# Two more chunks of the attention gate in the stage with seven half-size products

## The chip, the core and the metric

The kernel runs on one core of a Trainium2 chip. A core has TensorE (PE) for matrix products, VectorE (DVE), ScalarE (ACT) and GpSimd (POOL) for elementwise work, and SyncE (SP), whose queue issues most transfers. Products are written to PSUM, eight banks of 128 rows by 512 float32; the other operands lie in SBUF. The metric is the device time of one execution in microseconds. Before the change three runs gave a median of 717.32 us (716.94 to 717.59).

## The reference, cut to what matters

A decoder block on 1024 tokens and 16 meta tokens, width 1024, in float32. The normalised input h is projected at once into the pooling branch (u, its gate z), the attention (q, k, v, its gate za and forget logits f) and two gates of full width, g_pool and g_attn:

```python
h = rmsnorm(x, norm_g)
proj = jnp.einsum('bld,dn->bln', h, w_in)
u_pool, z_pool, q, k, v, z_attn, f_logit, g_pool, g_attn = jnp.split(proj, _split_points(), axis=-1)
y_pool = causal_multiscale_pool(u_pool, pool_w, pool_scale) * jax.nn.silu(z_pool)
y_attn = forgetting_attention(q, k, v, log_f).reshape(B, L, ATTN_WIDTH) * jax.nn.silu(z_attn)
merged = (jax.nn.sigmoid(g_pool) * jnp.einsum('blc,cd->bld', y_pool, w_up_pool)
          + jax.nn.sigmoid(g_attn) * jnp.einsum('blc,cd->bld', y_attn, w_up_attn))
return x + jnp.einsum('bld,de->ble', merged, w_out)
```

The gate projection g_attn has 1024 columns, eight chunks of 128. The case is where each of these chunks is computed.

## The kernel before, in words

Float32 operands are split into a high and a low part, and each product is made of three: high by high, high by low, low by high. A chunk of 128 columns over the 1024 tokens takes two halves of 512 tokens, each of 8 x 3 matmuls (`g_proj`, `g_mm3`, L221). Its weights come in one 512 KB load, are split by two instructions of ACT (L208) and four of POOL (L212), and `f_raw` evicts the result by ACT (L405) and stores it to DRAM (`spill`).

**Attention.** There are 16 units: four pairs of heads, two heads each, two halves of 512 queries. Units alternate between narrow ones (first half, five blocks of 128 keys) and wide ones (second half, nine). Per block, `qk` (L738, L739) makes the scores, ACT moves them out of PSUM (L743), VectorE keeps a running maximum (L752); `maxes` brings the maximum to all rows; `soft` subtracts it (L779), takes exp (L780), splits the result into high (L784, ACT) and low (L785, VectorE), and `av` (L803) multiplies both by V. `merged` interleaves the score steps of the next unit with the softmax steps of this one.

**Fill.** TensorE would wait in all of this, so a planner (`Fill`) puts other products between: the q, k and v projections of the next pair (which must be ready at the pair's boundary, `until`), and freely the four chunks of u, the eight of g_pool and chunks 0 to 3 of g_attn (`raws`). After every step it pulls matmuls worth `PACE * dve - pe`, with its own estimates of VectorE's and TensorE's time of the step; inside `maxes` and between the last steps it pulls fixed amounts (`LM1`, `LM2`, `LATENCY`). What is left when the last unit ends is drained. The order of TensorE is that of the program; the other engines are ordered by the scheduler in this part.

**The stage with seven products.** za, z and chunks 4 to 7 of g_attn are computed after it as one 1024 by 1024 by 1024 product cut into 2 x 2 blocks, by a scheme that takes seven products of half size in place of eight. Its weight matrix stands side by side from z and gate columns: in the left half za and gate chunks 4 and 5, in the right half z and gate chunks 6 and 7 (`GB`). Sums of its blocks are made ahead by DRAM copies and accumulating transfers (`GS`, 768 columns: 512 and 256), sums of h by `HS`. The list `order` names the chunks: product n of 0 to 6, chunk i of 0 to 5, with i below 4 for za and z and 4 and 5 for the gate. One entry (n, i) is 12 matmuls of 512 columns (L1079, `g_prod`). Step x of the loop splits the weights of entry x + 4 (`w_split`: ACT L1034, then POOL L1041 or, every third time, VectorE L1038), issues the product of entry x + 2, evicts entry x - 1 (`evict`, L1084, L1090), and does the extra work that `before` and `extra` name for the entry: softmax sums, pooling chains, the splits of h (L1050, L1055), the loads of the reciprocal sums (`rc_in`) and the division (`attn_norm`). All engines keep the program's order in this stage. Weights come in pairs of chunks, 512 KB each (`pairs`, L1022): two buffers hold them, from entry (2, 0) on two more. A buffer is free for the next load when both of its chunks are split. Gate results are kept in `XE` between products, staged in `st` and stored to DRAM; `g_flush` puts the stores on SP's queue at every third step. The last four entries follow the loop, in turn with the pooling's products (`pool_mm`).

After it come the two up-projections (`up`), which read the gates back from DRAM, and the output projection (L1405) in seven half-size products of its own.

Of the kernel before, what the change touches and what calls it, by code (L numbers as in the profile page):

```python
# [33 lines left out]
PACE = 1.32  # L34
LATENCY = 1800.0
LAT2 = 1600.0
LM1, LM2 = 1400.0, 3200.0
# [16 lines left out]
def tile_hybrid_block(ctx, tc, x, meta, norm_g, w_in, b_forget, pool_w, pool_scale,  # L54
# [93 lines left out]
    GS = {n: dr.tile([512, 768], F32, name=f"gs{n}") for n in (1, 2, 3, 4, 5)}  # L148
    GB = {f"{r + 1}{c + 1}": (w_in[0][512 * r:512 * r + 512, z:z + 512], w_in[0][512 * r:512 * r + 512, g:g + 256])
          for r in range(2) for c, (z, g) in enumerate(((COL_ZA, COL_GA + 512), (COL_Z, COL_GA + 768)))}  # L150
# [498 lines left out]
    for j in range(4, 8):  # L649
        spill["ga", j] = dr.tile([128, SEQ], F32, name=f"sp_ga{j}")  # L650
# [46 lines left out]
    def gsrc(n, q):  # L697
        if n in (2, 3, 5, 6):
            return GSRC[n][:, {"a": 0, "b": 256, "g": 512}[q]:][:, :256]
        return GSRC[n][1] if q == "g" else GSRC[n][0][:, 256 * (q == "b"):][:, :256]  # L700
# [134 lines left out]
    raws = [(n, j) for n, c in (("gp", 8), ("ga", 4)) for j in range(c)]  # L835
# [181 lines left out]
    def pairs_in():  # L1017
        while pairs and room:
            e = pairs.pop(0)
            homes[e] = tag = room.pop(0)  # L1020
            raw_w[e] = (wp if tag == "raw" else hq).tile([128, 4, 256], F32, name="graw", tag=tag)
            nc.sync.dma_start(raw_w[e], rows_of(gsrc(*e)))  # L1022
# [6 lines left out]
    def w_split(e):  # L1029
        n, i = e  # L1030
        raw = raw_w[n, "aabbgg"[i]][:, :, 128 * (i % 2):][:, :, :128]
        op = bp.tile([128, 2, 4, 128], F32R, name="gw", tag="y", bufs=6)
        op_w[e] = op
        ins = nc.scalar.activation(op[:, 0], raw, AF.Copy)  # L1034
        if not splits[0]:
            after(ins, evacs[-1])
        if splits[0] % 3 == 2:
            nc.vector.tensor_tensor(op[:, 1], raw, r32(op[:, 0]), op=ALU.subtract)  # L1038
        else:
            for k in (0, 2):  # L1040
                nc.gpsimd.tensor_tensor(op[:, 1, k:k + 2], raw[:, k:k + 2], r32(op[:, 0, k:k + 2]), op=ALU.subtract)  # L1041
        splits[0] += 1
# [22 lines left out]
    order = [(n, i) for n in range(7) for i in {5: (3, 2, 1, 0, 4, 5), 6: (4, 5, 3, 2, 1, 0)}.get(n, range(6))]  # L1065
# [47 lines left out]
    def evict(e):  # L1113
        n, i = e
        ps = onto[e]
        if i < 4:
            if n == 0:
                keep(za[i][:, T0_], ps)
            elif n == 1:
                plus_(za[i][:, T0_], ps)  # L1120
            elif n == 2:
                keep(zp[i][:, T0_], ps)
            elif n == 3:
                keep(zp[i][:, T1_], ps)
            elif n == 4:
                plus_(zp[i][:, T0_], ps)
                pool_tt(zp[i][:, T0_], zp[i][:, T0_], zp[i][:, T1_], ALU.add)
                defer(3, lambda: silu(zp[i][:, T0_], zp[i][:, T0_], -1.0))
            elif n == 5:
                plus_(zp[i][:, T1_], ps)  # L1130
                defer(1, lambda: silu(zp[i][:, T1_], zp[i][:, T1_], -1.0))
            else:
                silu(za[i][:, T1_], ps)
            return
        x, r = [t[:, i - 4] for t in XE]
        if n == 0:
            keep(x, ps)
        elif n in (1, 6):
            st = stage()
            plus_(st, ps, x)  # L1140
            g_store(i, T0_ if n == 1 else T1_, st)
        elif n == 2:
            plus_(x, ps)
        elif n == 3:
            keep(r, ps)
        elif n == 4:
            st = stage()
            plus_(st, ps, x)
            plus_(st, r)
            g_store(i + 2, T0_, st)  # L1150
        else:
            plus_(x, ps)
            pool_tt(r, r, x, ALU.add)
            g_store(i + 2, T1_, r)
# [4 lines left out]
    U = {}  # L1159
# [5 lines left out]
    pairs = [(0, "g")] + [(n, q) for n in range(1, 7) for q in {5: "bag", 6: "gba"}.get(n, "abg")]  # L1165
# [11 lines left out]
    def split_next(e):  # L1177
        w_split(e)
        q = e[0], "aabbgg"[e[1]]
        halves[q] = halves.get(q, 0) + 1  # L1180
        if halves[q] == 2:
# [18 lines left out]
    def steps_of(g):  # L1200
# [5 lines left out]
        (1, 3): [open_hq, lambda: h_split(2), lambda: pad_hq()],  # L1206
# [6 lines left out]
        (0, 4): [lambda: acc_sum(3)],  # L1213
# [12 lines left out]
        (3, 3): [lambda: pool_split(3), lambda: rc_in(0), lambda: rc_in(1)],  # L1226
# [4 lines left out]
        (4, 2): [lambda: rc_in(2)],  # L1231
        (4, 3): [lambda: attn_norm(0)],
        (4, 4): [lambda: attn_norm(1)],
        (4, 5): [lambda: pool_split(1), lambda: rc_in(3)],
        (5, 3): [lambda: h_split(6)],
        (5, 2): [lambda: attn_norm(2)],
        (5, 0): [lambda: silu(za[0][:, T0_], za[0][:, T0_])],
        (5, 4): [lambda: attn_norm(3), lambda: silu(za[1][:, T0_], za[1][:, T0_]),
                 lambda: silu(za[2][:, T0_], za[2][:, T0_])],
        (5, 5): [lambda: pool_split(0)],  # L1240
# [5 lines left out]
    for x, e in enumerate(order[:38]):  # L1246
# [3 lines left out]
        if 4 <= x + AH < 42:  # L1250
            split_next(order[x + AH])
        if x + 2 < 38:
# [3 lines left out]
        run_due(x)  # L1256
        if x:
            evict(order[x - 1])
        if x % 3 == 2:
            g_flush()  # L1260
# [264 lines left out]
```

## Time and profile before

| | |
|---|---|
| median of three runs | 717.32 us |
| profiled execution, its own time | 716.32 us |
| its span, first to last instruction | 714.6 us |
| TensorE busy | 705.5 us, 99% |
| VectorE, ACT, POOL busy | 73%, 59%, 48% |
| granted TensorE clock, mean | 0.997 |
| last attention product to the first product of the stage | 413.15 to 424.38 us |
| first product of the stage to the first pooling product | 424.38 to 528.04 us |

A group's row gives line, engine and operation, output from inputs, shape and count, then busy time, mean duration in ns, and the idle time of the engine before it with what ended it. A matmul's busy time runs to its modelled end and overlaps the next, so that the rate of matmuls is read from their starts. A row of the timeline begins with start and duration in us.

### The profile page before, as it was taken

The numbers are of one execution on the slowest core, as the hardware profiler recorded it, in microseconds if no ns is written. First come the engines' busy times: TensorE is split into PE (matmuls) and PEld (weight loads), VectorE is DVE, ScalarE is ACT, GpSimd is POOL, SyncE is SP. The second block draws the span as 40 slices with busy tenths as digits, with TensorE's granted clock in tenths as the row PEclk, the third lists the DMA queues.
The fourth block names the chain that finished last, engine by engine and source line by source line (L and its number), as shares of the span: only waits on it lengthen the run. The fifth ranks groups of instructions, "written<-read, shape, count | busy, mean of one in ns | idle before, by whom it ended". The sixth has DMA issues, their size and how long they took to land.

```text
span 714.6 us, 10896 instructions
## 1 busy us (share of the span) xinstructions
PE 705.5 (99%) x3613; PEld 609.5 (85%) x3613; DVE 520.2 (73%) x916; ACT 420.4 (59%) x928; POOL 345.8 (48%) x465
## 2 busy tenths in 40 slices
PE   8999999999999999999999999999999999999996
PEld 6997999998899888898888888888888888888885
DVE  5784488576788867797677847986957554988775
ACT  7663577676767778777676623446556332535445
POOL 5413447476285837656297743355972011007152
PEclk9999999999999999999999999999999999999998
DMA  9459977956534485455656459689917466761006
GB/s 307 128 198 373 323 270 178 217 123 155 113 106 100 133 220 119 133 133 111 170 169 201 108 191 350 181 221 288 269 45 262 130 231 220 262 236 60 0 1 235
DMA packets 95354, 129.89 MB, mean 182 GB/s; under 512 B 11457, under 2 KB 62657, under 8 KB 93266
## 3 DMA queue, kind: packets, MB, share of 16 engines
q1 hardware_dynamic: 91776, 110.32, 48.2%
q0 software_dynamic: 2224, 16.25, 12.2%
q10 hardware_dynamic: 1298, 2.63, 1.0%
q8 instruction: 28, 0.46, 0.3%
q14 instruction: 28, 0.23, 0.1%
HBM read 102.25 MB, written 58.39 MB: 225 GB/s over the span
## 4 chain that ended last, share of the span: by engine, by line
PE 92%; DVE 4%; ACT 2%; issue 1%; POOL 0%; POOLq 0%; ACTq 0%; DVEq 0%
PE pj L221 52%; PE pj L1079 12%; PE pj L1405 8%; PE po L803 5%; PE pt L1079 4%; PE pt L1405 2%; PE ps L739 2%; PE ps L738 2%; PE pj L599 1%; DVE pl L785 1%; PE pj L739 1%; PE pt L283 1%; PE pj L738 1%; ACT qa L319 1%; DVE ql L323 1%
## 5 line engine op out<-in xcount | busy, mean ns | idle before, releaser
L221 PE MATMUL pj<-hh,whi 128*128 128x512 f32 (+3 forms) x576 | 127.1, 347 | 0.6 <-DVE ql L323 0.3
L221 PE MATMUL pj<-hh,wlo 128*128 128x512 f32 (+3 forms) x576 | 127.2, 346 | 0.0
L221 PE MATMUL pj<-hl,whi 128*128 128x512 f32 (+3 forms) x576 | 126.8, 345 | 0.0
L212 POOL TENSOR_TENSOR wlo<-raw,whi 128x256 fp32r<-128x256 f32 x100 | 76.1, 791 | 65.4 <-ACT whi L208 34.5
L221 PEld LDWEIGHTS pj<-hh,whi 128*128 128x128 f32 x576 | 97.2, 188 | 11.3 <-ACT hh L285 0.5
L221 PEld LDWEIGHTS pj<-hh,wlo 128*128 128x128 f32 x576 | 96.8, 188 | 10.0
L221 PEld LDWEIGHTS pj<-hl,whi 128*128 128x128 f32 x576 | 96.5, 188 | 9.7
L793 POOL TENSOR_TENSOR acc<-acc,S 128x256 f32<-128x256 f32 (+2 forms) x128 | 90.6, 727 | 8.3 <-ACT S L780 4.4
L785 DVE TENSOR_TENSOR pl<-S,ph 128x512 fp32r<-128x512 f32 (+4 forms) x112 | 80.0, 736 | 15.6 <-ACT ph L784 15.3
L1041 POOL TENSOR_TENSOR gw<-graw,gw 128x256 fp32r<-128x256 f32 x52 | 49.1, 968 | 50.1 <-ACT gw L1034 41.9
L1079 PE MATMUL pj<-gh,gw 128*128 128x512 f32 x276 | 64.3, 389 | 0.0
L1079 PEld LDWEIGHTS pj<-gh,gw 128*128 128x128 f32 x276 | 51.8, 188 | 10.8
L752 DVE TENSOR_TENSOR pt<-pt,S 128x400 f32<-128x400 f32 (+2 forms) x96 | 46.6, 485 | 19.7 <-ACT S L743 17.6
L780 ACT ACTIVATE S<-S 128x512 f32<-128x512 f32 (+4 forms) x112 | 50.2, 481 | 12.7 <-DVE S L779 12.5
L784 ACT ACTIVATE ph<-S 128x512 fp32r<-128x512 f32 (+4 forms) x112 | 52.5, 482 | 3.2 <-PE po L803 2.2
L779 DVE TENSOR_TENSOR S<-S,pt 128x512 f32<-128x512 f32 (+4 forms) x112 | 50.0, 499 | 0.6
L1034 ACT ACTIVATE gw<-graw 128x512 fp32r<-128x512 f32 x38 | 23.3, 624 | 33.6 <-DMA graw<-gs 20.2
L1297 DVE TENSOR_TENSOR rl<-pj,rl 128x512 f32<-128x512 f32 x32 | 22.0, 689 | 27.7 <-PE pj L221 27.4
L793 POOL TENSOR_TENSOR acc<-S 128x256 f32<-128x256 f32 (+1 forms) x32 | 29.5, 948 | 23.6 <-ACT S L780 20.5
L743 ACT ACTIVATE S<-ps,negc 128x16 f32<-128x16 f32 (+4 forms) x65 | 33.0, 513 | 11.5 <-PE ps L739 10.9
L803 PE MATMUL po<-ph,V 128*128 128x512 f32 (+4 forms) x112 | 36.4, 325 | 0.0
L1405 PE MATMUL pj<-opw 128*128 128x512 f32 (+1 forms) x168 | 36.2, 374 | 0.0
(250 smaller groups left out, 1395.9 us busy)
## 6 DMA issues: line engine op xcount, KB each, us to landing
raw<-in_w_in_dram SPq DMA_DIRECT2D x27, 512.0 KB, 6.2
gs<-in_w_in_dram SPq DMA_DIRECT2D x15, 512.0 KB, 8.3
gs<-gs POOLq DMA_DIRECT2D x4, 1536.0 KB, 13.0
graw<-gs SPq DMA_DIRECT2D x12, 512.0 KB, 8.3
td<-in_w_out_dram SPq DMA_DIRECT2D x10, 512.0 KB, 9.9
graw<-in_w_in_dram SPq DMA_DIRECT2D x9, 512.0 KB, 5.7
xt<-in_x_dram SPq DMA_DIRECT2D x8, 512.0 KB, 6.4
accd<-acc SPq DMA_DIRECT2D x16, 256.0 KB, 2.5
```

What stands on the lines that cost most here:

```text
L212: ins = nc.gpsimd.tensor_tensor(lo[:, k:k + 2], raw[:, k:k + 2], r32(hi[:, k:k + 2]), op=ALU.subtract)
L221: nc.tensor.matmul(ps, a, b, start=(i == 0), stop=(i == len(seq) - 1))
L752: nc.vector.tensor_tensor(m[:kb, c0:], m[:kb, c0:], s[:kb, c0:], op=ALU.max)
L779: nc.vector.tensor_tensor(s[:kb, c0:], s[:kb, c0:], self.pm[:kb, c0:], op=ALU.subtract)
L780: exps.append(nc.scalar.activation(s[:kb, c0:], s[:kb, c0:], AF.Exp))
L784: nc.scalar.activation(ph[:kb, c0:], s[:kb, c0:], AF.Copy)
L785: dves.append(nc.vector.tensor_tensor(pl[:kb, c0:], s[:kb, c0:], r32(ph[:kb, c0:]), op=ALU.subtract))
L793: accs.append(nc.gpsimd.tensor_tensor(acc[:kb, c:c1], (S0 if b == 1 else acc)[:kb, c:c1], s[:kb, c:c1], op=ALU.add))
L803: nc.tensor.matmul(self.po[:, c0:], v, self.P[b][i][:kb, c0:], start=(b == 0 and i == 0), stop=(b == self.nb - 1 and i == 1))
L1041: nc.gpsimd.tensor_tensor(op[:, 1, k:k + 2], raw[:, k:k + 2], r32(op[:, 0, k:k + 2]), op=ALU.subtract)
L1079: nc.tensor.matmul(ps, stat(n, i, p, k), op_h[n][q][k // 2][:, k % 2], start=fresh and m == 0, stop=m == 11, skip_group_check=True)
L1405: nc.tensor.matmul(ps, pick(A_, k, p)[:, i * 128:(i + 1) * 128], pick(B_, k, q)[:, c0:c1], start=start and n == 0, stop=n == 11, skip_grou ...
```

## The change

Gate chunks 2 and 3 leave the fill and join the stage: `GB` and `GS` grow from 768 to 896 columns, with gate chunks 2 to 4 in the left half and 5 to 7 in the right. Each of the seven products gets a seventh entry i = 6, loaded by itself in a 256 KB piece `"e"` that takes a buffer alone. Its partial results live in one more tile of the pool `g` (`X6`), which also serves as its stage. The planner's `PACE` goes from 1.32 to 1.2 and `LM2` from 3200 to 2600. Stores are flushed at each step, ahead of the eviction. Some extra work is named for other entries: the loads of the reciprocal sums come later, as does the last division, and the last pooling split goes behind the loop. The gate's signs in `up` follow the new halves.

```diff
-PACE = 1.32
+PACE = 1.2
-LM1, LM2 = 1400.0, 3200.0
+LM1, LM2 = 1400.0, 2600.0
...
-    GS = {n: dr.tile([512, 768], F32, name=f"gs{n}") for n in (1, 2, 3, 4, 5)}
-    GB = {f"{r + 1}{c + 1}": (w_in[0][512 * r:512 * r + 512, z:z + 512], w_in[0][512 * r:512 * r + 512, g:g + 256])
-          for r in range(2) for c, (z, g) in enumerate(((COL_ZA, COL_GA + 512), (COL_Z, COL_GA + 768)))}
+    GS = {n: dr.tile([512, 896], F32, name=f"gs{n}") for n in (1, 2, 3, 4, 5)}
+    GB = {f"{r + 1}{c + 1}": (w_in[0][512 * r:512 * r + 512, z:z + 512], w_in[0][512 * r:512 * r + 512, g:g + 384])
+          for r in range(2) for c, (z, g) in enumerate(((COL_ZA, COL_GA + 256), (COL_Z, COL_GA + 640)))}
...
     def gsrc(n, q):
+        c0, w = {"a": (0, 256), "b": (256, 256), "g": (512, 256), "e": (768, 128)}[q]
         if n in (2, 3, 5, 6):
-            return GSRC[n][:, {"a": 0, "b": 256, "g": 512}[q]:][:, :256]
-        return GSRC[n][1] if q == "g" else GSRC[n][0][:, 256 * (q == "b"):][:, :256]
+            return GSRC[n][:, c0:c0 + w]
+        return GSRC[n][1][:, c0 - 512:c0 - 512 + w] if q in "ge" else GSRC[n][0][:, c0:c0 + w]
...
-    raws = [(n, j) for n, c in (("gp", 8), ("ga", 4)) for j in range(c)]
+    raws = [(n, j) for n, c in (("gp", 8), ("ga", 2)) for j in range(c)]
...
-    order = [(n, i) for n in range(7) for i in {5: (3, 2, 1, 0, 4, 5), 6: (4, 5, 3, 2, 1, 0)}.get(n, range(6))]
+    order = [(n, i) for n in range(7) for i in {5: (3, 2, 1, 0, 4, 5, 6), 6: (4, 5, 6, 3, 2, 1, 0)}.get(n, range(7))]
...
-        x, r = [t[:, i - 4] for t in XE]
+        x, r = [t[:, i - 4] for t in XE] if i < 6 else [X6[0][:, T0_], X6[0][:, T1_]]
         if n == 0:
             keep(x, ps)
         elif n in (1, 6):
-            st = stage()
+            st = stage() if i < 6 else (r if n == 1 else x)
             plus_(st, ps, x)
-            g_store(i, T0_ if n == 1 else T1_, st)
+            g_store(i - 2, T0_ if n == 1 else T1_, st)
...
-    pairs = [(0, "g")] + [(n, q) for n in range(1, 7) for q in {5: "bag", 6: "gba"}.get(n, "abg")]
+    pairs = [(n, q) for n in range(7) for q in {0: "ge", 5: "bage", 6: "geba"}.get(n, "abge")]
...
-        (1, 3): [open_hq, lambda: h_split(2), lambda: pad_hq()],
+        (1, 4): [open_hq, lambda: h_split(2), lambda: pad_hq()],
...
-        (0, 4): [lambda: acc_sum(3)],
+        (0, 4): [lambda: X6.append(gp.tile([128, SEQ], F32, name="gxe", tag="g")), lambda: acc_sum(3)],
...
-        (3, 3): [lambda: pool_split(3), lambda: rc_in(0), lambda: rc_in(1)],
+        (3, 3): [lambda: pool_split(3)],
+        (3, 6): [lambda: rc_in(0), lambda: rc_in(1)],
...
-        (4, 2): [lambda: rc_in(2)],
-        (4, 5): [lambda: pool_split(1), lambda: rc_in(3)],
+        (4, 5): [lambda: pool_split(1)],
+        (4, 6): [lambda: rc_in(2)],
-        (5, 2): [lambda: attn_norm(2)],
+        (5, 2): [lambda: attn_norm(2), lambda: rc_in(3)],
-        (5, 4): [lambda: attn_norm(3), lambda: silu(za[1][:, T0_], za[1][:, T0_]),
+        (5, 4): [lambda: silu(za[1][:, T0_], za[1][:, T0_]),
-        (5, 5): [lambda: pool_split(0)],
+        (5, 6): [lambda: attn_norm(3)],
...
         run_due(x)
+        g_flush()
         if x:
             evict(order[x - 1])
-        if x % 3 == 2:
-            g_flush()
...
-        evict((6, i + 1) if n else (6, 5))
+        evict((6, i + 1) if n else (6, 6))
+        if n == 0:
+            pool_split(0)
```

More of the change, by code (lines that the diff above doesn't have):

```diff
@@ L647, in tile_hybrid_block @@
         spill["y", p] = dr.tile([128, SEQ if p == 3 else 2 * SEQ], F32, name=f"sp_y{p}")
-    for j in range(4, 8):
+    for j in range(2, 8):
         spill["ga", j] = dr.tile([128, SEQ], F32, name=f"sp_ga{j}")
@@ L1020, in pairs_in @@
             homes[e] = tag = room.pop(0)
-            raw_w[e] = (wp if tag == "raw" else hq).tile([128, 4, 256], F32, name="graw", tag=tag)
+            raw_w[e] = (wp if tag == "raw" else hq).tile([128, 4, 128 if e[1] == "e" else 256], F32, name="graw", tag=tag)
             nc.sync.dma_start(raw_w[e], rows_of(gsrc(*e)))
@@ L1030, in w_split @@
         n, i = e
-        raw = raw_w[n, "aabbgg"[i]][:, :, 128 * (i % 2):][:, :, :128]
+        raw = raw_w[n, "aabbgge"[i]][:, :, 128 * (i % 2):][:, :, :128]
         op = bp.tile([128, 2, 4, 128], F32R, name="gw", tag="y", bufs=6)
@@ L1149, in evict @@
             plus_(st, r)
-            g_store(i + 2, T0_, st)
+            g_store(i + 1, T0_, st)
         else:
@@ L1153, in evict @@
             pool_tt(r, r, x, ALU.add)
-            g_store(i + 2, T1_, r)
+            g_store(i + 1, T1_, r)
     for i in range(4):
@@ L1158, in tile_hybrid_block @@
     XE = [bp.tile([128, 2, 512], F32, name=n, tag="xe", bufs=2) for n in ("gx", "ge")]
-    U = {}
+    U, X6 = {}, []
     def u_in(g):
@@ L1178, in split_next @@
         w_split(e)
-        q = e[0], "aabbgg"[e[1]]
+        q = e[0], "aabbgge"[e[1]]
         halves[q] = halves.get(q, 0) + 1
-        if halves[q] == 2:
+        if halves[q] == (1 if q[1] == "e" else 2):
             room.append(homes[q])
@@ L1245, in tile_hybrid_block @@
         split_next(e)
-    for x, e in enumerate(order[:38]):
+    for x, e in enumerate(order[:45]):
         if x == 0:
@@ L1249, in tile_hybrid_block @@
             g_prod(order[1])
-        if 4 <= x + AH < 42:
+        if 4 <= x + AH < 49:
             split_next(order[x + AH])
-        if x + 2 < 38:
+        if x + 2 < 45:
             g_prod(order[x + 2])
@@ L1286, in up @@
         wh, wl = ws[:2]
-        ins = nc.scalar.activation(sg_, sg_, AF.Sigmoid, scale=-1.0 if a and j > 5 else 1.0)
+        ins = nc.scalar.activation(sg_, sg_, AF.Sigmoid, scale=-1.0 if a and j > 4 else 1.0)
         after(ins, evacs[-1])
```

## The prediction

> **What bounds the kernel now.** I read the page's totals first, then the busy times by stage, then TensorE's own order of time, then what the side engines wait for.
>
> ```profile
> span 714.6 us, 10896 instructions
> PE 705.5 (99%) x3613; PEld 609.5 (85%) x3613; DVE 520.2 (73%) x916; ACT 420.4 (59%) x928; POOL 345.8 (48%) x465
> L221 PE MATMUL pj<-hh,whi 128*128 128x512 f32 (+3 forms) x576 | 127.1, 347 | 0.6 <-DVE ql L323 0.3
> L1079 PE MATMUL pj<-gh,gw 128*128 128x512 f32 x276 | 64.3, 389 | 0.0
> ```
>
> TensorE is busy 99% of the span, and its two largest groups waited 0.6 us together. By stage (columns: busy PE, weight loads, DVE, ACT, POOL, clock, DMA share, GB/s), the attention, the fill left behind it, the gate stage, one wide and one narrow attention unit:
>
> ```profile
> 60.00:413.00 353.00, 352.80 (x1896) 315.11 (x1894) 263.67 (x569) 246.64 (x614) 210.35 (x290) 1.00 0.64 169
> 413.00:424.40 11.40, 11.40 (x54) 9.45 (x53) 6.60 (x6) 1.79 (x3) 3.37 (x3) 1.00 0.59 186
> 424.40:528.00 103.60, 103.60 (x457) 85.61 (x456) 80.99 (x79) 51.95 (x82) 59.88 (x62) 1.00 0.79 238
> 191.50:207.50 16.00, 16.00 (x77) 13.51 (x76) 15.12 (x26) 14.49 (x33) 13.56 (x17) 1.00 0.41 105
> 168.90:185.00 16.10, 16.10 (x79) 13.43 (x77) 9.13 (x20) 11.48 (x25) 6.41 (x11) 1.00 0.67 171
> ```
>
> No stage leaves TensorE idle. VectorE is 75% busy over the attention, but 15.12 of 16.00 us in the softmax of a wide unit (nine key blocks) and 9.13 of 16.10 in a narrow one (five). So the bound is TensorE's stream everywhere, and the nearest other limit is VectorE in the wide units.
>
> **The price of a matmul.** A busy matmul overlaps its neighbours, so I price by the distance of starts:
>
> ```profile
> 413.15 0.48 PE L221 MATMUL pj<-hh,wlo 128*128 128x512 f32 x1
> 413.46 2.01 PE L221 MATMUL pj<-hh,whi 128*128 128x512 f32 x8
> 422.57 1.98 PE L221 MATMUL pj<-hh,wlo 128*128 128x512 f32 x8
> 424.38 1.07 PE L1079 MATMUL pj<-hh,gw 128*128 128x512 f32 x4
> 528.04 0.39 PE L221 MATMUL pj<-plh,pwh 128*128 128x512 f32 x1
> ```
>
> From 413.46 to 424.38 run 48 matmuls, the last chunk of the gate (two halves of 24): 10.92 us, 227.5 ns each. It stands behind the last attention product, as pure drain. From 424.38 to 528.04 run the 38 half-size products of the loop, 456 matmuls: 103.66 us, 227.3 ns each, 2.73 us a product. The Trainium skill (TensorE: Matmul & The Clock Gate, section Back-to-back issue gap) gives N/2.4 + 2.5 ns, 216 ns at 512 columns, for a lone stream, and about 131 ns for sustained pairs of weight load and matmul; by the second the net below would be 12 × 0.131 = 1.6 us, but the 227 ns of this trace lie by the first, and the measurement decides.
>
> **The change, part by part.** *Removed from the fill:* chunks 2 and 3, 2 × 48 = 96 matmuls, 2 × 10.92 = 21.84 us; with them two 512 KB weight loads, four splits on ACT, eight on POOL, four evictions and their stores, all beside TensorE's work. *Added to the gate stage:* a seventh product in each of the seven, 7 × 12 = 84 matmuls, 84 × 0.2273 = 19.09 us. **Net on TensorE: −2.75 us.** Beside it the gate stage gains seven splits, nine passes over evicted tiles and seven 256 KB loads (as many stores as the fill had):
>
> ```profile
> L1038 DVE TENSOR_TENSOR gw<-graw,gw 128x512 fp32r<-128x512 f32 x12 | 10.5, 877 | 5.4 <-ACT gw L1034 5.4
> L1041 POOL TENSOR_TENSOR gw<-graw,gw 128x256 fp32r<-128x256 f32 x52 | 49.1, 968 | 50.1 <-ACT gw L1034 41.9
> L1090 DVE TENSOR_TENSOR zp<-pj,zp 128x512 f32<-128x512 f32 x6 | 3.8, 679 | 1.9 <-PE pj L1079 1.9
> L1034 ACT ACTIVATE gw<-graw 128x512 fp32r<-128x512 f32 x38 | 23.3, 624 | 33.6 <-DMA graw<-gs 20.2
> L976 DVE TENSOR_TENSOR pll<-u,plh 128x1024 fp32r<-128x1024 f32 x4 | 6.5, 1615 | 1.2 <-ACT plh L975 1.2
> ```
>
> VectorE: three more splits (every third is its own) and six adds, 3 × 0.877 + 6 × 0.679 = 6.7 us. POOL: four splits of two and one add of two, 10 × 0.968 = 9.7 us. ACT: seven splits and two evictions, about 9 × 0.624 = 5.6 us. The stage grows by 19.1 us, so each lies beside TensorE: 0. If that cover failed, the longest, POOL's, would cost up to 9.7 us.
>
> *The moved steps.* The division row of head pair 2 is loaded two products ahead of its use instead of five:
>
> ```profile
> rc<-recs SPq DMA_DIRECT2D x8, 256.0 KB, 6.1
> ```
>
> Two products are 5.5 us, so VectorE may wait about 0.6 us, with evictions queued behind whose banks TensorE wants again several products later: 0, at worst 0.6. The last pooling split goes into the tail, ACT and VectorE (1.6 us), three turns of 18 matmuls (4.1 us each) ahead of its use: 0, at worst 1.6. Flushing stores at each step puts SP's weight loads behind more waits for evictions; I take that up with the loads below. The bigger copies and sums through DRAM (896 columns for 768) have the attention as cover.
>
> **What pays for it: the pace.** Two of the planner's constants fall, so that less fill is spread over all units. I followed its sums in the code (fill pulled = pace × VectorE estimate − own matmuls). For before they leave 49 matmuls to the drain, as the rows above show (1 + 48). For after they leave 26. A narrow unit then carries about 11.8 us of planned fill for 13.2, a wide one 13.8 for 15.4; one wide unit at a head-pair boundary carries 24.6 for 15.5, since the next pair's values must be ready. So TensorE arrives at each wide unit's second products earlier: 0.6 us from the shorter wait after the maxima, and 0.12 (1.32 − 1.2) of the 7.3 us that the planner estimates for the blocks passed by the sixth, 0.9 us; together 1.5 us there, and 1.8 at the unit's end. Whether it then waits is read from the lead of VectorE there. The low part of the sixth block (400 columns) and the matmul that reads it, in three wide units:
>
> ```profile
> 287.04 0.62 DVE L785 TENSOR_TENSOR pl<-S,ph 128x400 fp32r<-128x400 f32 x1
> 287.80 0.37 PE L803 MATMUL po<-pl,V 128*128 128x400 f32 x1
> 204.63 1.06 DVE L785 TENSOR_TENSOR pl<-S,ph 128x400 fp32r<-128x400 f32 x1
> 206.68 0.34 PE L803 MATMUL po<-pl,V 128*128 128x400 f32 x1
> 366.89 0.93 DVE L785 TENSOR_TENSOR pl<-S,ph 128x400 fp32r<-128x400 f32 x1
> 370.99 0.34 PE L803 MATMUL po<-pl,V 128*128 128x400 f32 x1
> 284.61 1.39 DVE L323 SCALAR_TENSOR_TENSOR ql<-pj,qa 64x512 fp32r<-64x512 f32 x2 [1.50 <-ACT qa L319]
> ```
>
> The leads are 0.14, 0.99 and 3.17 us. Less 1.5, they become stalls of 1.4 and 0.5 us and a lead of 1.7: 1.9 us if these two alone fall short and their fill stays as it is. It doesn't: the tightest comes from VectorE standing 1.50 us behind a query chunk of the fill, and the planner now puts that chunk wholly into the narrow unit before. Bounds: 0 (no stall, all leads rearranged) and 4 us (both stalls, and 0.3 us in each of the six other wide units). I take 1.0, nearer the low end, as the largest stall loses its cause. A narrow unit leaves VectorE 7 us, which covers its loss.
>
> **Sum.** The profiled execution took 716.32 us, 1.7 beyond its span and 1.0 under the median of 717.32. 716.32 − 2.75 + 1.0 = 714.57; with the 1.0 to the median, **715.5 us**.
>
> **The rivals.** *A, the sum as it stands:* stalls under 1.3 us, about 715.5. For it: every lead but two that I show is longer than what is taken.
>
> *B, the stalls eat the gain:* 1.3 to 4.2 us of them, mid 2.7, time 717.3. For it: the two short leads as they are (1.9 us). Against it: the moved query chunk.
>
> *C, slower: VectorE becomes the bound in the wide units.* It has 0.88 us free in 16.00 there, and 1.5 are taken. Should the fill's new places leave four of the wide units without a lead, each stalls 1.5 us: 6.0, time 717.32 − 2.75 + 6.0 = 720.6. It decides from 4.2 us of stalls in all. Its durations can grow too:
>
> ```profile
> L785 DVE TENSOR_TENSOR pl<-S,ph 128x512 fp32r<-128x512 f32 x48 | 44.1, 937 | 13.5 <-ACT ph L784 13.4
> L1276 DVE TENSOR_TENSOR wlu<-rawu,whu 128x512 fp32r<-128x512 f32 x15 | 10.2, 683 | 0.0
> ```
>
> The same subtraction takes 937 ns beside a busy POOL and 683 beside an idle one. The Trainium skill (SBUF — State Buffer, section Who interferes with whom) says that a VectorE operation with two SBUF inputs and a GpSimd one that reads SBUF exclude each other; the two rows agree, and by it a denser attention makes VectorE's operations longer. Against C: narrow units reset the lead.
>
> *D, the gate stage's loads come late.* The single chunk takes a whole one of two buffers, so until two more open there are four loads per 19.1 us instead of three per 16.4:
>
> ```profile
> ACT gw L1034 <- DMA graw<-gs: 20.2, 6, 5.8
> 473.01 0.63 ACT L1034 ACTIVATE gw<-graw 128x512 fp32r<-128x512 f32 x1 [5.80 <-DMA graw<-gs]
> 479.08 3.11 PE L1079 MATMUL pj<-gh,gw 128*128 128x512 f32 x13
> SPq L1000 <- DMA sums<-ge: 9.2, 1, 9.2
> ```
>
> ACT already waited 5.80 us for one load, and its split ended 5.4 us before its product (479.08). Each round of four loads loses up to 2.7 us of that, twice before the buffers open, and the read of the softmax sums then holds SP's queue for 9.2 us, the later loads behind it: 0 stall if the lead was 5.4 or more, some 4 us if all stood in a row, 718.6 with A's 1.0. I take 0.
>
> **Chances.** A 0.47, B 0.26, C 0.16, D 0.11, of which half ends within 0.2% (1.43 us, about what a measurement of this kernel tells from no change) and half above. So faster (under 715.9) 0.47, within 0.31, slower (over 718.8) 0.22. The likeliest is A. The range runs from 713.9, A without a stall and half a microsecond of scatter, to 720.3, just short of C's price.
>
> **What would show it.** Right: fill matmuls 96 fewer, gate matmuls 84 more at 2.73 us a product, drain of 26. The stalls would stand as idle time before the second attention products, released by VectorE or ACT, in wide units. D would stand as idle time before gate products released by a split. Wrong: idle TensorE over 4 us in either stage, or the distance of starts moving off 227 ns.

## The result and the profile after

The changed kernel takes 723.81 us (median of 4 runs, 722.95 to 724.13) against 717.13 (716.38 to 717.59) for the kernel before beside it: ratio 1.0092, 95% interval 1.0075 to 1.011. It is slower; I had forecast 715.5 us with 713.9 to 720.3, and the time lies above the range. Lines behind the function `gsrc` are one higher than before (L803 is now L804, L1079 is L1080).

The totals of the changed kernel's page:

```profile
span 721.2 us, 10911 instructions
PE 706.5 (98%) x3601; PEld 606.5 (84%) x3601; DVE 521.7 (72%) x925; ACT 419.2 (58%) x929; POOL 346.5 (48%) x467
```

Twelve matmuls fewer, as planned, and a span 6.6 us longer. The busy times of the changed kernel by stage (columns as in the prediction: attention, rest of the fill, gate loop to the first pooling product):

```profile
60.00:407.00 347.00, 341.44 (x1830) 302.18 (x1828) 261.15 (x570) 241.40 (x609) 203.58 (x283) 1.00 0.66 174
407.00:411.46 4.46, 4.46 (x21) 3.67 (x20) 4.36 (x5) 0.00 (x0) 0.00 (x0) 1.00 0.95 295
411.46:534.18 122.72, 122.72 (x542) 101.42 (x541) 85.74 (x88) 56.70 (x90) 71.46 (x74) 1.00 0.75 229
```

In the attention TensorE now stands idle for 347.00 − 341.44 = 5.56 us, where it was 0.2; over 4 us was the sign that the prediction had named against itself. The gate loop has no idle time at all. Its two ends on TensorE, in order of time:

```profile
411.46 1.07 PE L1080 MATMUL pj<-hh,gw 128*128 128x512 f32 x4
...
534.16 0.40 PE L221 MATMUL pj<-plh,pwh 128*128 128x512 f32 x1
```

With the same two rows of before (424.38 and 528.04) the 6.6 us divide cleanly. *The gate loop* takes 122.70 us for 103.66: +19.04. *Behind it* lie 721.2 − 534.16 = 187.04 us, 186.56 before: +0.5. *Ahead of it* its first product starts 12.92 us earlier; the 96 matmuls that left the fill are worth 21.84, so 8.92 us were lost there. −12.92 + 19.04 + 0.5 = +6.6. Below, "lost before the stage" is this quantity: the start of the stage's first product, less 424.38 us, plus 21.84 where two chunks have left the fill. (The part ahead of the attention is in it too: the first score product starts at 82.69 us before and between 82.23 and 83.72 in the other profiled executions, so that two of them can differ by 1.5 us before the attention begins.)

TensorE's waits in the attention of the changed kernel (engine, output and line, what it waited for: us in all, times, longest):

```profile
PE pj L739 <- ACT S L744: 1.6, 1, 1.6
PE po L804 <- ACT ph L785: 1.0, 1, 1.0
PE ps L739 <- DVE ka L342: 1.0, 1, 1.0
PE pj L221 <- DVE ka L342: 0.7, 1, 0.7
PE pj L739 <- DVE S L748: 0.5, 1, 0.5
PE ps L739 <- ACT S L744: 0.5, 1, 0.5
```

The view shows idle time only. By the distances of starts, in which a wait isn't shortened by the modelled end of the matmul before it, 14 stalls of 0.14 to 1.79 us make 7.9 us of the 8.92; the kernel before has one, of 0.37. I sort them by what TensorE waited for: *score products* (L739) for a bank whose evictions (L744, L748) are late, 7 stalls, 3.8 us, of which two, 1.3 us near 95 and 101 us, turn out below to be the work of the transfers; *key chunks of the fill* (the next matmuls wait for VectorE's L342), 2 stalls, 2.0 us; *the first products of wide units* (L804, high part from ACT L785), 2 stalls, 1.3 us; *the second products* (low part from VectorE L786), 2 stalls, 0.5 us; and one of 0.25 behind V's split (L367). The prediction had priced the fourth kind, the second products, alone.

Four places of the changed kernel in order of time. First the fourth kind, the one of the prediction, in the wide unit whose lead was 0.99 us (204.63 in the prediction's rows):

```profile
196.55 0.56 DVE L786 TENSOR_TENSOR pl<-S,ph 128x400 fp32r<-128x400 f32 x1
...
197.16 0.45 PE L804 MATMUL po<-pl,V 128*128 128x400 f32 x1
```

The matmul starts 0.05 us after its operand, so the lead lost 0.94 us, and TensorE had stalled 0.39 us here and 0.14 two products earlier: 1.47 us together, the 1.5 that the prediction took for such a unit.

Second, a key chunk:

```profile
226.10 1.16 PE L221 MATMUL pj<-hh,wlo 128*128 128x272 f32 x8
227.94 1.11 PE L221 MATMUL pj<-hh,whi 128*128 128x384 f32 x5 [0.68 <-DVE ka L342]
230.02 0.47 PE L739 MATMUL ps<-qa,ka 128*128 128x512 f32 x1 [0.96 <-DVE ka L342]
...
226.67 1.12 DVE L342 TENSOR_TENSOR ka<-pj,ka 64x384 fp32r<-64x384 f32 x2
227.83 1.52 DVE L780 TENSOR_TENSOR S<-S,pt 128x512 f32<-128x512 f32 x3
229.38 0.96 DVE L342 TENSOR_TENSOR ka<-pj,ka 64x256 fp32r<-64x256 f32 x3
```

The chunk's own evictions stand in VectorE's queue between softmax passes of a new unit (L780), and the next piece and the next score product want their banks. From 224 to 232 us VectorE is busy 7.02 of 8.00 us, ACT 7.28 and POOL 7.50:

```profile
224.00:232.00 8.00, 6.35 (x41) 5.74 (x40) 7.02 (x16) 7.28 (x18) 7.50 (x10) 1.00 0.72 211
```

Over the whole unit (220.1 to 244.5 us) VectorE is busy 19.36 of 24.40 us, ACT 17.31 and POOL 16.00; over these 8 us all three are nearly full.

Third, the wide unit whose lead was the shortest, 0.14 us (287.04 there):

```profile
274.70 2.41 ACT L319 ACTIVATE qa<-pj 64x512 fp32r<-64x512 f32 x4
277.01 0.62 ACT L785 ACTIVATE ph<-S 128x512 fp32r<-128x512 f32 x1
...
279.86 0.50 PE L804 MATMUL po<-ph,V 128*128 128x512 f32 x1 [0.98 <-ACT ph L785]
```

The query chunk that stood ahead of VectorE in the middle of this unit (284.61 in the prediction's rows) is in another place, as the prediction said, but that place is ACT's queue at the start of the same unit: 2.41 us ahead of the first high part. In the kernel before, that place held another query chunk, which followed the first two high parts instead of preceding them:

```profile
273.09 0.63 ACT L784 ACTIVATE ph<-S 128x512 fp32r<-128x512 f32 x1
...
274.67 0.61 ACT L784 ACTIVATE ph<-S 128x512 fp32r<-128x512 f32 x1
275.19 2.39 ACT L319 ACTIVATE qa<-pj 64x512 fp32r<-64x512 f32 x4
```

TensorE now stalls 1.29 us in two pieces, 0.14 and 1.15.

Fourth, the largest, in a narrow unit:

```profile
370.10 3.06 POOL L212 TENSOR_TENSOR wlo<-raw,whi 128x256 fp32r<-128x256 f32 x4
373.11 1.40 POOL L794 TENSOR_TENSOR acc<-S 128x256 f32<-128x256 f32 x2
374.59 2.59 POOL L794 TENSOR_TENSOR acc<-acc,S 128x256 f32<-128x256 f32 x4
...
371.80 4.30 DVE L786 TENSOR_TENSOR pl<-S,ph 128x512 fp32r<-128x512 f32 x2
376.27 0.22 ACT L781 ACTIVATE S<-S 128x16 f32<-128x16 f32 x1 [3.23 <-DVE S L780]
378.20 0.50 PE L739 MATMUL pj<-qa,ka 128*128 128x512 f32 x1 [1.62 <-ACT S L744]
```

Two of VectorE's subtractions take 4.30 us; by the single records the first of them takes 3.27, and no other of this line in either kernel takes over 1.3. It stands beside a train of POOL operations without a gap. ACT waits 3.23 us for VectorE's next pass, its own eviction (L744) comes late, and TensorE stalls 1.79 us. The Trainium skill (SBUF — State Buffer, section Who interferes with whom) says that a VectorE operation with two SBUF inputs contends with a GpSimd one that reads SBUF, for a pair of ports that is locked exclusively. The trace agrees as far as the subtraction is long beside POOL's train: it lasted while five POOL operations began (372.20 to 374.59 us). How long such a wait can last that section doesn't say, and no run here separates the ports from another cause.

### The profile page after: what moved, and what is told of

It is laid out like the page before. It is cut to its first block, busy times and chain, and to the rows that moved or that the text cites. A ratio compares the mean times of both kernels' runs of the same rounds, so it can differ in the third digit from the quotient of the medians.

```text
span 721.2 us, 10911 instructions
## 1 busy us (share of the span) xinstructions
PE 706.5 (98%) x3601; PEld 606.5 (84%) x3601; DVE 521.7 (72%) x925; ACT 419.2 (58%) x929; POOL 346.5 (48%) x467
## 4 chain that ended last, share of the span: by engine, by line
PE 84%; DVE 7%; ACT 3%; DMA 2%; issue 2%; POOL 1%; POOLq 0%; SPq 0%; ACTq 0%
PE pj L221 43%; PE pj L1080 14%; PE pj L1408 8%; PE pt L1080 5%; PE po L804 5%; PE pt L1408 2%; DMA raw<-in_w_in_dram 2%; PE ps L740 1%; PE ps L739 1%; DVE S L780 1%; PE pj L599 1%; DVE pl L786 1%; PE pt L283 1%; PE pj L739 1%; ACT qa L319 1%
## 5 line engine op out<-in xcount | busy, mean ns | idle before, releaser
L221 PE MATMUL pj<-hh,whi 128*128 128x512 f32 (+3 forms) x544 | 121.1, 346 | 1.0 <-DVE ka L342 0.7
L221 PE MATMUL pj<-hl,whi 128*128 128x512 f32 (+3 forms) x544 | 119.4, 343 | 0.0
L221 PE MATMUL pj<-hh,wlo 128*128 128x512 f32 (+3 forms) x544 | 117.5, 342 | 0.0
L212 POOL TENSOR_TENSOR wlo<-raw,whi 128x256 fp32r<-128x256 f32 x92 | 68.9, 805 | 74.7 <-ACT whi L208 58.5
L221 PEld LDWEIGHTS pj<-hh,whi 128*128 128x128 f32 x544 | 90.7, 188 | 10.6 <-PE pj L221 0.9
L221 PEld LDWEIGHTS pj<-hh,wlo 128*128 128x128 f32 x544 | 90.7, 188 | 8.4
L786 DVE TENSOR_TENSOR pl<-S,ph 128x512 fp32r<-128x512 f32 (+4 forms) x112 | 77.2, 709 | 11.5 <-ACT ph L785 11.2
L1042 POOL TENSOR_TENSOR gw<-graw,gw 128x256 fp32r<-128x256 f32 x60 | 56.0, 959 | 48.8 <-ACT gw L1035 45.8
L1080 PE MATMUL pj<-gh,gw 128*128 128x512 f32 x312 | 72.8, 389 | 0.0
L1080 PEld LDWEIGHTS pj<-gh,gw 128*128 128x128 f32 x312 | 58.6, 188 | 12.2
L785 ACT ACTIVATE ph<-S 128x512 fp32r<-128x512 f32 (+4 forms) x112 | 52.2, 484 | 2.4 <-PE po L804 1.4
L780 DVE TENSOR_TENSOR S<-S,pt 128x512 f32<-128x512 f32 (+4 forms) x112 | 50.1, 498 | 0.7
L1298 DVE TENSOR_TENSOR rl<-pj,rl 128x512 f32<-128x512 f32 x32 | 22.0, 688 | 27.6 <-PE pj L221 27.3
L744 ACT ACTIVATE S<-ps,negc 128x512 f32<-128x512 f32 (+4 forms) x67 | 33.8, 512 | 8.0 <-PE ps L740 7.7
L804 PE MATMUL po<-ph,V 128*128 128x512 f32 (+4 forms) x112 | 36.8, 329 | 1.0 <-ACT ph L785 1.0
## 6 DMA issues: line engine op xcount, KB each, us to landing
gs<-gs POOLq DMA_DIRECT2D x4, 1792.0 KB, 13.8
td<-in_w_out_dram SPq DMA_DIRECT2D x10, 512.0 KB, 10.8
```

The source lines that it names most:

```text
L212: ins = nc.gpsimd.tensor_tensor(lo[:, k:k + 2], raw[:, k:k + 2], r32(hi[:, k:k + 2]), op=ALU.subtract)
L221: nc.tensor.matmul(ps, a, b, start=(i == 0), stop=(i == len(seq) - 1))
L780: nc.vector.tensor_tensor(s[:kb, c0:], s[:kb, c0:], self.pm[:kb, c0:], op=ALU.subtract)
L785: nc.scalar.activation(ph[:kb, c0:], s[:kb, c0:], AF.Copy)
L786: dves.append(nc.vector.tensor_tensor(pl[:kb, c0:], s[:kb, c0:], r32(ph[:kb, c0:]), op=ALU.subtract))
L804: nc.tensor.matmul(self.po[:, c0:], v, self.P[b][i][:kb, c0:], start=(b == 0 and i == 0), stop=(b == self.nb - 1 and i == 1))
```

## The experiments

All ratios are against the kernel before, run beside them. The third column is defined above; the stage is from its first product to the first pooling product; the fill is what the planner's sums give a narrow and a wide unit.

| kernel | ratio, 95% interval | lost before the stage | stage | fill, us |
|---|---|---|---|---|
| before | 1 | 0 | 103.66 | 13.2, 15.4 |
| after | 1.0092 (1.0075 to 1.011) | 8.9 | 122.70 | 11.8, 13.8 |
| before, both constants | 1.0104 (1.0086 to 1.0122) | 8.7 | 103.66 | 11.8, 13.8 |
| before, PACE 1.2 alone | 1.0092 (1.0063 to 1.0121) | 4.7 | 103.66 | 12.3, 14.4 |
| before, LM2 2600 alone | 1.0048 (1.0029 to 1.0067) | 2.6 | 105.90 | 12.6, 14.7 |
| before, wider copies | 1.0063 (1.0038 to 1.0088) | 4.0 | 105.89 | 13.2, 15.4 |
| before, five early copies | 1.000 (0.9987 to 1.0013) | 0.6 | 103.66 | 13.2, 15.4 |
| after, chunks also in the fill | 1.0298 (1.0278 to 1.0318) | 3.7 | 122.70 | 13.2, 15.4 |
| after, old constants | 1.0077 (1.0054 to 1.0101) | 6.9 | 124.55 | 13.2, 15.4 |
| after, five early copies | 1.0072 (1.0045 to 1.0098) | 7.4 | 122.70 | 11.8, 13.8 |
| after, 1.35 and 2400 | 1.0006 (0.9997 to 1.0016) | 3.8 | 122.69 | 12.6, 14.8 |
| after, values in parts, 1.32 and 2800 | 1.006 (1.0038 to 1.0081) | 7.7 | 122.73 | 12.7, 15.1 |
| the same, five early copies | 1.0032 (1.002 to 1.0044) | 5.8 | 122.73 | 12.7, 15.1 |
| after, 1.35 and 2400, five early copies | 0.9983 (0.9968 to 0.9998) | 3.0 | 122.69 | 12.6, 14.8 |
| after, 1.35 and 2400, three early copies | 0.9976 (0.9961 to 0.9991) | 2.1 | 122.69 | 12.6, 14.8 |
| after, 1.28 and 2800, five early copies | 0.9983 (0.9968 to 0.9998) | 3.8 | 122.71 | 12.5, 14.7 |
| after, 1.38 and 2200, five early copies | **0.9971 (0.9956 to 0.9985)** | 1.6 | 122.79 | 12.5, 14.9 |

Two theories stood against each other. *P*: the stalls come from the lower pace and the new places of the fill. *T*: they come from the transfers, the copies through DRAM of 896 columns for 768.

**The constants alone, on the kernel before.**

```diff
-PACE = 1.32
+PACE = 1.2
-LM1, LM2 = 1400.0, 3200.0
+LM1, LM2 = 1400.0, 2600.0
```

> The kernel before with only the planner's two constants changed (PACE 1.2, LM2 2600); four gate chunks stay in the fill, the stage and the copies stay as they were. By the planner's sums 122 matmuls (27.7 us) are then left to the drain. Theory P (the lower pace makes the stalls: TensorE comes to the softmax's results before they are ready): the attention stalls as in the changed kernel, about 8 us more than before, so 725 us (722 to 727), the stalls as idle time ahead of score and second attention products. Theory T (the wider copies and sums through DRAM, or the stage, make them): neither is changed here, so 717 us.

Measured 725.45 us. P holds: with no chunk moved and no copy widened, 8.7 us are lost, and most stalls stand where the changed kernel has them; those near 95 and 101 us are missing. In their stead the clock fell here after the two waits at the key chunk, 0.64 and 0.96 us of idle time (windows of this kernel; the column behind POOL's is the granted clock):

```profile
226.00:228.00 2.00, 1.11 (x5) 0.82 (x5) 1.94 (x5) 1.93 (x7) 2.00 (x4) 1.00 1.50 493
228.00:232.00 4.00, 3.61 (x12) 3.45 (x13) 1.49 (x7) 2.79 (x8) 3.92 (x7) 0.62 0.29 70
```

The mean clock of these 4 us was 0.62; by windows of 1 us it stood at 0.50 from 229 to 232, and at 0.98 and 0.81 in the windows next to them. Nine matmuls from the score product behind the wait (228.39 to 231.25) took 2.86 us; the same nine in the changed kernel (230.02 to 231.84) took 1.82 at full clock. By the time the clock was back, the same stretch had taken 4.24 us here (to 232.63) and 2.70 there (to 232.72): 1.5 of the 8.7 us are the half clock's, and 7.2 are left for the waits.

**Each constant by itself.** The first alone, and the second alone, on the kernel before.

> Edit: the kernel before with the first constant alone as in the kernel after (1.2 for 1.32; 3200 stays), no other change; 113 matmuls are left to the drain instead of 49, which costs TensorE nothing by itself. If the lower pace between the blocks makes most of the 8 us that both constants cost on this kernel: 722 to 724 (ratio 1.007 to 1.009). By the prediction's split (0.9 us of lead in a wide unit of 1.5 is the pace's): 4.8 us of the 8, ratio 1.0065.

> Edit: the kernel before with the second constant alone as in the kernel after (2600 for 3200; 1.32 stays); 58 matmuls left to the drain. By the prediction's split (0.6 us of lead in a wide unit of 1.5): 3.2 us of the 8, ratio 1.0045. If the losses come only where both leads are used up together: under 1.002.

Measured 722.96 and 720.52 us, ratios 1.0092 and 1.0048. Before the stage they lose 4.7 and 2.6 us, near the 4.8 and 3.2 of the prediction's split; the total of the first is above it, with a wide interval. The second loses another 2.2 us in the gate stage of its profiled execution, on which see below, so that the fit of its total (1.0048 for 1.0045) is in part luck. Together the two lose 7.3 us, close to the 7.2 of waits that both constants cost at once. With the table's last column this is one series: less fill in a pair of units (28.6, 27.3, 26.7, 25.6 us), more lost (0, 2.6, 4.7, 8.7). Both have a stall near 102 us (0.95 and 0.49 us) without wider copies, so a stall at that place isn't by itself a sign of the copies.

**The old constants on the kernel after.**

```diff
-PACE = 1.2
+PACE = 1.32
-LM1, LM2 = 1400.0, 2600.0
+LM1, LM2 = 1400.0, 3200.0
```

> The changed kernel with the old constants (PACE 1.32, LM2 3200). Theory P: up to the fourteenth unit no more stalls than before; then the fill has run dry (9.9 us of planned fill missing in the last wide unit) and TensorE waits there for VectorE, about 7 us, all of it after 385 us: 717.1 - 2.75 + 7 = 721 us (719 to 723), no drain. Theory T: the 8 us of stalls stay where they were in the changed kernel, and the dry end comes on top: 729 us.

Measured 723.66 us, between the two. The stalls up to the fourteenth unit are three near 97 to 104 us, 1.4 us together, and the one that the kernel before has too. With two chunks fewer, the fill runs dry in the last unit at the old pace, about 9.9 us too little by the planner's sums:

```profile
403.00:409.00 6.00, 3.97 (x11) 2.27 (x11) 5.89 (x12) 4.31 (x12) 5.84 (x8) 0.79 0.12 45
409.00:413.00 4.00, 4.00 (x12) 3.25 (x12) 3.94 (x5) 0.59 (x1) 2.54 (x4) 0.50 0.12 43
```

TensorE is busy 3.97 of 6.00 us, and then runs at a clock of 0.50 for 4 us, which lengthens the gate stage by 1.9 us. So the fill per unit has to fall with the removal; that `PACE` itself has to isn't shown, and the best kernels below have it at 1.35 and 1.38. The Trainium skill (TensorE: Matmul & The Clock Gate, section Part 1: The HAM clock gate) puts the half clock behind an idle window of about 3.4 us; the rows show the half clock, but no wait of that length: by starts the two waits ahead of it here are of 2.0 and 0.9 us, and in the run with both constants there were two, of 0.64 and 0.96 us idle.

**The stage alone.** Chunks 2 and 3 are computed in the stage and also, as before, in the fill; the constants are the old ones.

```diff
-raws = [(n, j) for n, c in (("gp", 8), ("ga", 2)) for j in range(c)]
+raws = [(n, j) for n, c in (("gp", 8), ("ga", 4)) for j in range(c)]
```

> The changed kernel's stage with seven entries, but the fill and the pace of before: chunks 2 and 3 of the gate are computed twice, once as fill and once in the stage (whose results are the ones used). Theory P: the stage itself has no stall and costs its 84 matmuls, 19.1 us: 717.1 + 19.1 = 736.2 us (735.5 to 737), attention as in the kernel before. Theory T: the wider copies or late loads stall TensorE: 738 us or more.

Measured 739.56 us, 21.9 over before. The stage is 19.04 us longer without a stall, so rival D is false and the moved steps cost nothing. The other 3 us lie in the attention, whose fill is that of before, so T isn't nothing. Three stalls (1.4 us) lie between 96 and 104 us, the place that T names. The longest, 1.43 us, lies at 144.38, behind a store of the fill's results that ACT had to wait for:

```profile
143.26 0.49 ACT L416 ACTIVATE st<-pj 128x384 f32<-128x384 f32 x1 [3.91 <-DMA sp_u<-st]
```

The kernel with the old constants, whose fill and copies are the same there, has no such stall, so that this one is the copies' isn't shown.

**The copies alone.** On the kernel before, GS has 896 columns; 128 of them are copied and summed and read by nobody.

```diff
-GS = {n: dr.tile([512, 768], ...
+GS = {n: dr.tile([512, 896], ...
-w_in[0][512 * r:512 * r + 512, g:g + 256])
+w_in[0][512 * r:512 * r + 512, g - 128:g + 256])
...
```

The lines left out make the loads skip the 128 new columns.

> Edit: the kernel before, with the copies and sums through DRAM 896 columns wide instead of 768, of which the gate stage reads the same 768 as before; 128 columns are copied and summed and read by nobody. No matmul and no place of the fill changes. Theory T: the third raw weight load of the attention's first units lands late behind the bigger copies on its queue, TensorE stalls 1.4 to 3 us between 95 and 103 us, time 719 to 720.5. If the pace alone makes all stalls (P): 717.3, as before.

Measured 721.95 us, with single runs from 718.71 to 725.07; the profiled one took 723.43. T is larger than it expected. ACT's order of time at the first unit's maxima, in this kernel,

```profile
90.91 1.15 ACT L208 ACTIVATE whi<-raw 128x512 fp32r<-128x512 f32 x2 [5.31 <-DMA raw<-in_w_in_dram]
```

in the kernel before,

```profile
86.46 1.15 ACT L208 ACTIVATE whi<-raw 128x512 fp32r<-128x512 f32 x2 [1.06 <-PE pj L221]
```

and in the changed one, with the score product that waits later:

```profile
88.67 1.15 ACT L208 ACTIVATE whi<-raw 128x512 fp32r<-128x512 f32 x2 [3.42 <-DMA raw<-in_w_in_dram]
...
95.60 0.50 PE L739 MATMUL ps<-qa,ka 128*128 128x512 f32 x1 [0.46 <-ACT S L744]
```

A weight load issued near 75 us stands on SP's queue behind the copies. It lands at 85.21 us in the kernel before, at 88.56 in the changed one and at 90.80 here, 3.4 and 5.6 us later, and the split starts 2.2 and 4.5 us later. Its split waits at the head of ACT's queue, and the maxima and exponentials of the first unit wait behind it. In this run 4.0 us are lost before the stage and 2.2 in it. That second loss is rival D's mechanism, in the *old* order of the stage. The kernel with the second constant alone has it too:

```profile
483.80 4.36 PE L1079 MATMUL pj<-gh,gw 128*128 128x512 f32 x18 [1.96 <-DVE gx L1090]
...
480.37 0.63 ACT L1034 ACTIVATE gw<-graw 128x512 fp32r<-128x512 f32 x1 [6.12 <-DMA graw<-gs]
```

A load of a weight sum comes late: its split starts 53.38 us into the stage, where that of the kernel before (473.01 in the prediction's rows) starts after 48.63. VectorE's work follows, and TensorE stalls. No profiled execution of the new order shows such a stall; what decides whether the old one falls into it I haven't settled.

**Fewer early copies.** Nine copies are issued right ahead of the attention; here five, the others later at the loads that follow. On the kernel after, and on the one before.

```diff
-    copies(9)
+    copies(5)
```

> Edit: the kernel after, with five instead of nine copies issued ahead of the first weight loads of the attention, nothing else. Theory T for the two stalls at 95 and 101 us alone: these 1.3 us go, the others (7.7 us) stay, time about 722 (721 to 723). Theory T as the main cause: under 720. Theory P alone: as the kernel after, 723.8.

> Edit: the kernel before with five instead of nine copies ahead of the attention's first weight loads, nothing else. Its first weight loads are in time as they are, so the same time as before (ratio 0.999 to 1.001): then the gain of the kernels that have the change, the new constants and fewer copies is the change's. If the copies cost the kernel before too: 0.9975, and the change itself has gained nothing.

Measured 722.35 and 717.42 us. The changed kernel loses 1.5 us less (7.4 for 8.9), and in the trace the stalls at 95 and 101 us are gone:

```profile
86.90 1.15 ACT L208 ACTIVATE whi<-raw 128x512 fp32r<-128x512 f32 x2 [1.30 <-issue]
```

The split no longer waits for the load. The kernel before gains nothing. So T is real, about a sixth of the loss, and P the larger part. By these numbers the terms add up in the changed kernel: the 7.2 us of waits that the constants cost alone and the 1.5 that the copies cost make 8.7 of its 8.9. With the old constants T costs more, 3.7 to 4.0; that a stall gives the side engines their lead back, so that one loss stands in for another, would explain it, but isn't shown.

**The fill spread.** On the kernel after, the constants 1.35 and 2400: by the planner's sums one matmul is left for the drain instead of 26, and 18.0 us of fill instead of 24.6 in the unit ahead of the pair boundary.

> The changed kernel with PACE 1.35 and LM2 2400: by the planner's sums 1 matmul instead of 26 is left to the drain, the lump of the eighth unit falls from 24.6 to 18.0 us of fill, and narrow and wide units get 12.6 and 14.9 us in place of 11.8 and 13.8 (13.2 and 15.4 before). Theory P: the leads at the sixth block of wide units lose 0.6 instead of 1.5 us, stalls of about 2 us remain: 717.1 - 2.75 + 2 = 716.4 us (715.3 to 718). Theory T: as the changed kernel, 723 us.

Measured 718.21 us, just above P's range. 5.1 of the 8.9 us are back, with the wider copies in place; the gain of 2.8 stays hidden under 3.8 that are still lost.

**Values in parts.** The pair's last transposes may stand anywhere instead of in one piece.

```diff
-F.add(f"v{p}", v_blocks(p, 6, 7, 8, 0), 4 * p - 2, apart=True)
+F.add(f"v{p}", v_blocks(p, 6, 7, 8, 0), 4 * p - 2)
```

> Edit: the kernel after with the pace constants 1.32 and 2800 and with the values' entry of the planner as parts that may stand anywhere before their due time, not as one part in one unit. The planner's sums then are: 2 matmuls left to the drain, narrow units 12.7 us of fill, wide ones 15.1, no unit with 24.6. Theory P (the stalls are the price of the places and the lower pace of the fill): the leads lose only about 0.4 us against before, so the nine or more stalls of the kernel after (7.5 us) go, and what is left are the ones at 95 and 101 us; time 717.3 - 2.75 + about 1.5 = 716 (714.7 to 717.5). Theory T (the wider copies through DRAM are the main cause): the stalls of before 110 us stay and others with them, time above 719.

> Edit: the kernel of the run with the values' entry in parts and the constants 1.32 and 2800, and five instead of nine copies issued ahead of the first weight loads of the attention; the rest of the copies follow where they did. Both theories together (P for the stalls later on, T for those at 95 and 101 us): the load of 74 us lands by 86 instead of 88 us, no stall before 110 us, time 714.5 to 716, 1.3 to 2 us under the same kernel with nine copies. If the copies are no cause: the same time as with nine.

Measured 721.77 and 719.70 us, well above both forecasts. The units carry more fill than in the kernel after, and the pace stalls shrink, but the transposes now follow their chunk at once and wait for its eviction (kernel with nine copies):

```profile
PE pj L359 <- ACT vt L347: 1.4, 1, 1.4
...
PE ps L359 <- ACT vt L347: 1.3, 1, 1.3
```

By starts these are 1.5 us each, and 0.3 at a third place. The sum of fill isn't all; what stands next to what counts as much. Fewer copies take off 2.1 us here.

**Both repairs.** Constants as named and `copies(5)` or `copies(3)`, nothing else.

> Edit: the kernel after with the constants 1.35 and 2400 (the fill spread without rest to the drain) and five instead of nine copies issued ahead of the attention's first weight loads. If the losses of the pace and of the copies are two independent terms: the run with the constants alone (1.0006 of before), less the 1.5 to 2.0 us that the fewer copies took off two other kernels: 0.9982 of before, 715.5 to 716.5 us at 717.3 before. If the copies' stalls only move on: 1.000 or more.

> Edit: the kernel after with the constants 1.35 and 2400 and three instead of nine copies ahead of the attention's first weight loads. If each copy ahead of the load costs its share: 0.3 to 0.7 us less than with five, about 715.5. If five are already few enough that the load is in time: the same as with five. If the copies come too late for the sums through DRAM later on: slower.

> Edit: as the run with 1.35, 2400 and five copies, but with the constants 1.28 and 2800: the same fill in sum (7 matmuls to the drain), more of it after the maxima and less between the blocks of the softmax. If the stalls hang on the sum of fill in a unit only: the same time as with 1.35 and 2400. If they hang on the lead in the blocks, as the prediction had it: 0.04 x 7.3 to 0.07 x 8.5 us less lead at the later blocks of a wide unit, stalls there, 1 to 4 us more.

> Edit: as the run with 1.35, 2400 and five copies, but with the constants 1.38 and 2200: the same fill in sum, less of it after the maxima and more between the blocks. If the lead in the blocks decides: 0 to 1 us faster than 1.35 and 2400. If the wait after the maxima decides (the first exponentials are not ready when the fill after the maxima ends): stalls of 0.2 us in each unit ahead of the first product with the values, 1 to 3 us slower.

Measured 716.92, 716.55, 717.18 and 716.45 us, against 717.80 (35 runs of before, 716.02 to 721.78). All four are a little below the kernel before by their medians; the fastest, 1.38 and 2200, has a ratio of 0.9971 (0.9956 to 0.9985). The first has the ratio that two independent terms gave (0.9983 for 0.9982). Against the scatter of before, three or five copies and the division between the two constants make no difference beyond the intervals. Compared with each other, the 12 runs with 1.38 and 2200 (715.95 to 716.93) lie mostly under the 12 with 1.28 and 2800 (716.70 to 717.89), so a little more fill in the blocks helps; the medians differ by 0.7 us. The 1 to 4 us that 1.28 and 2800 was to cost against 1.35 and 2400, if the lead in the blocks decides, came out as 0.3. In the column lost before the stage, 1.6 against 3.8, the greater part lies ahead of the attention; from the first score product on it is 2.1 against 2.7. The fastest one's attention and stage:

```profile
60.00:406.00 346.00, 344.88 (x1855) 307.54 (x1853) 263.76 (x570) 245.13 (x611) 201.72 (x283) 1.00 0.67 179
406.00:545.40 139.40, 139.40 (x615) 114.77 (x613) 101.67 (x106) 61.81 (x100) 82.13 (x84) 1.00 0.73 219
```

TensorE is idle 1.12 us in the first row, where the changed kernel had 5.56. With 1.6 us lost before the stage and 0.7 behind it the sum is −21.84 + 19.13 + 1.6 + 0.7 = −0.4 us, the difference of the profiled spans (714.2 and 714.6); by the medians it is 1.35 us. Much of that is the scatter of before: the shortest runs of the two kernels, 715.95 and 716.02, differ by 0.07 us, and the long ones, up to 721.78, belong to before alone.

## Why the prediction failed

**Right.** The removal (21.84 us) and the addition (19.04 measured, 19.09 forecast) stand: net −2.80 for −2.75. The side work of the stage, the loads and the moved steps cost 0, as the run with the stage alone shows. The drain is 26 matmuls, as forecast. Where a second product met a short lead, the loss was 1.47 us for 1.5, and each constant by itself cost about what the split gave it before the stage (4.7 and 2.6 us, 4.8 and 3.2 of 8). The last is partly luck: the split was worked out for the lead of the second products, and most of what was lost lies at other places. Two slips in the adding up change nothing: 714.57 and 1.0 make 715.6, and the lower end of the range comes to 714.1.

**Wrong: the stalls from the lower pace, taken as 1.0 us with bounds 0 and 4.** Measured: 8.9 us lost before the stage, and 8.7 from the two constants alone, 7.2 of them waits. Three steps failed, two of this term and one of the copies, which the sum had put at nothing.

*Only one kind of place was looked at.* I read the lead of one product, the low part of the sixth block, in three wide units, and from that I set the bounds. That kind gave 0.5 us. Score products behind their evictions gave 3.8 (1.3 of them the copies'), key chunks 2.0, the first products of a unit 1.3. "A narrow unit leaves VectorE 7 us" was true of the unit it was read from and did not help: the largest stall is in a narrow unit.

*"The largest stall loses its cause."* The query chunk moved from VectorE's way to the start of the unit in ACT's way, and cost 1.29 us where 1.4 had been struck out.

*"The bigger copies and sums through DRAM (896 columns for 768) have the attention as cover."* TensorE is covered; a weight load on the same queue is not. Undone by itself this is 1.5 us of the loss, and with the old constants 3.7 to 4.0.

**The rivals.** C had the sign and the point of decision (over 4.2 us), and its mechanism was half right: VectorE's late work does hold TensorE, but not because VectorE fills the wide units as a whole. At the key chunk all three side engines are nearly full for 8 us; at the largest stall POOL is (7.43 of 8.00 us from 370 to 378), with VectorE at 6.51 and ACT at 4.56. C's 6.0 us were short by 2.9. D was false in the new order of the stage.

**What remains open.** The 14 stalls, less the one of the kernel before, make 7.5 of the 8.9 us; the other 1.4 I haven't assigned. What decides whether waits bring the half clock is open too. That it comes in some runs of a kernel and not in others is suggested by their mean granted clocks: with the old constants on the kernel after, three runs at 0.992 took 722.88 to 724.62 us and one at 0.999 took 721.81; with five early copies alone, two at 0.994 and 0.995 took 723.38 and 723.18, and two at 0.997 and 0.998 took 721.52 and 721.39.

## What to carry to other kernels

Fill that a bound engine computes in another engine's shadow is also that engine's spacing: before taking some out, read the lead of every kind of consumer (first and second products, score banks, the evictions of the fill itself), not only the one with the shortest row. When fill is removed, keep the fill per unit near its old value and let the drain and the lumps shrink instead; here 12.5 and 14.9 us a unit in place of 11.8 and 13.8, with the drain at nearly nothing and five early copies, gave back the most. A transfer is covered only if what stands behind it on its queue is covered too.

## What the runs showed of the hardware

In two profiled executions waits of 1 to 2 us on TensorE were followed by half its clock: 0.50 for some 3.4 us after two waits of 0.64 and 0.96 us idle, and for some 6.8 us (406.5 to 413.3) after waits of 2.0 and 0.9 us by starts. In the first case that cost another 1.5 us; after like waits in the changed kernel's profiled execution the clock stayed at 1.00. A VectorE subtraction with both inputs in SBUF took 3.27 us beside an unbroken train of POOL operations; in the run with the lower pace alone two at the same place took 3.39 us together, and in the kernel before the first one of that unit took 0.67. A 512 KB weight load issued behind nine copies on the same queue landed 10.8 us after its issue in the kernel before, 14.0 and 15.4 us with the wider copies (changed kernel, and copies alone), and 7.4 us behind five of the wider copies.
